# Retention gates and outputs with tokens on the partitions

## The chip, the cores and the metric

One core of one Trainium2 chip runs the whole program. The metric is device time in microseconds (us). Five engines work side by side, each in the order of its own instruction list: TensorE (PE in the profile, its weight loads PEld), VectorE (DVE), ScalarE (ACT), GpSimd (POOL) and SyncE (SP), which here only issues DMAs.

## The reference

Two layers over 256 tokens of 2048 features; layer 0 mixes tokens by retention, layer 1 by a short convolution, and each is followed by a SwiGLU. Everything is float32. What the change touches is the retention mixer:

```python
def retention_mixer(h, cos, sin, w_in, w_out):
    q, k, v, g = jnp.split(h @ w_in, [qk_w, 2 * qk_w, 2 * qk_w + v_w], axis=-1)
    q = rope(split_heads(q, RET_HEADS), cos, sin)
    k = rope(split_heads(k, RET_HEADS), cos, sin) * (RET_DK ** -0.5)
    v = split_heads(v, RET_HEADS)
    ...
    o = rms_norm(chunked_gated_linear_attention(q, k, v, log_a))
    o = merge_heads(o).astype(h.dtype)
    return ((jax.nn.silu(g) * o) @ w_out).astype(h.dtype)
```

There are 8 heads, with 256 features for q and k and 512 for v and g. The norm runs over the 512 outputs of one head and one token.

## The kernel before

**Layout.** Activations lie with features on the partitions and tokens along the free dimension: a tile of 128 features by 256 tokens. Float32 products are made from two rounded parts, `hi` (the value rounded) and `lo` (the rest), so one product takes three terms: hi x hi, hi x lo, lo x hi. `h[k]` holds both parts of feature block k.

**Weights.** All matrices lie in one array in the order of their use. `fetch` loads 1 MB pieces over SP's queue; `prepare` turns half a piece (1024 columns) into `hi` on ACT (L310) and `lo` on DVE (L313); `take` hands out the next 128 columns (512 for v). Up to two halves are prepared ahead, in four buffers each for `hi` and `lo`. TensorE streams through these pieces for nearly the whole span.

**Products.** A unit is one block of 128 weight columns for one k. `product` uses two matmuls per unit (L355 with 512 columns, L358 with 256). `packed` puts two column blocks in the two halves of one PSUM bank and uses three matmuls of 256 columns (L378 to L380); the weights stand still in the array and the tokens stream. `values` makes v the other way: the tokens stand still (two halves of 128) and 512 weight columns stream (L806 to L808), so that v comes out with tokens on the partitions. There are eight banks, each of 128 partitions by 512 values, and every call of `bank()` takes one.

**Retention.** While the modulation of layer 0 is still being computed, four spans (`SPANS`) already add up some k of q, k and g for heads 0 to 4 (19 to 191 us); `held` copies those sums to `ahead`. Then `projections` runs for the heads in the order 4, 0, 2, 1, 5, 3, 6, 7: q, k, v, `scores`, and the gates g in two groups of two column blocks, with SiLU on ACT (`gate`). After four heads, and after eight, `ret_out` multiplies by the output matrix.

**Asides.** The rest of a head, `mixed`, is cut into four steps that are put into TensorE's list between the units of the next head (or of `ret_out`): after 8, 8, 24 and 12 units (`STEPS`). `outputs(0)` and `outputs(1)` make two blocks each of 128 output features: four matmuls a block (L852, L855), `summed` (ACT copies one half of the bank, DVE adds the other: L387, L389), squares (ACT, L404, and DVE, L405), and a product with the gate (L860). `roots` sums the squares over the partitions on TensorE (L413), a small DVE operation takes the mean (L422), and POOL raises it to the power -1/2 (L424). `ends` spreads the factor over the partitions with TensorE (L431), multiplies (L869), and splits the result into `hi` and `lo` (L394 on ACT, L395 on DVE) as `mid`, the input of the output product.

**Order.** TensorE's list is in program order throughout. Outside of the start, the other engines' lists are ordered by the framework, which also puts in the waits. The rows of the modulation matrix are loaded and reduced on DVE (L244, 2.3 us each) at a pace that `paced` sets, with low priority.

Of the kernel before, what the change touches and what calls it, by code (L numbers as in the profile page):

```python
# [17 lines left out]
P = 128  # L18
# [27 lines left out]
MOD_LEAD = 64  # L46
MOST = 0.045
MOD_PRIO = -300
STEPS = (8, 8, 24, 12)
RAW_BUFS = 3  # L50
PART_BUFS = 4

# [4 lines left out]
class Group:  # L57


    def __init__(self, cols, width=P, ks=range(KT)):  # L60
        self.cols, self.width, self.ks = cols, width, list(ks)


def ret_in_groups():

    qkg, v = [], []
    for h in range(HEADS):  # L70
        q = [Q0 + h * DK + i * P for i in range(2)]
        k = [K0 + h * DK + i * P for i in range(2)]
        g = [G0 + h * DV + i * P for i in range(4)]
        qkg.append([q, k, g[:2], g[2:]])
        v.append(Group([V0 + h * DV], DV))
    done = [0] * HEADS
    spans = []
    for heads, (a, b) in SPANS:
        assert all(done[h] == a for h in heads)
        for h in heads:  # L80
            done[h] = b
        spans.append(Group([c for h in heads for pair in qkg[h] for c in pair], ks=range(a, b)))
# [73 lines left out]

def laid_out(arrays):

    total = sum(len(g.cols) * g.width * len(g.ks) for _, _, g in in_use_order())
    out = np.empty((total // CHUNK, P, CHUNK), np.float32)  # L160
    at = 0
    for key, i, g in in_use_order():
        for k in g.ks:
            for c in g.cols:
                o = at % CHUNK
                out[at // CHUNK, :, o : o + g.width] = arrays[key][i, k * P : (k + 1) * P, c : c + g.width]
                at += g.width
    assert at == total and total % CHUNK == 0
    return out

# [15 lines left out]
def trunk(ctx: ExitStack, tc: tile.TileContext, x_in, c_in, pos_in, w_mod, cols_in, tab_in, w_all, out):  # L186
# [75 lines left out]
    first = len(RET_SPANS[0].cols) * FIRST_KS  # L262
    early = sum(len(g.cols) * len(g.ks) for g in RET_SPANS)
    plan_mod = [(early, 0), (1024, 18), (1984, 49), (5184, 9 * KT), (5888, n_mod)]
    units, allowed = [0], [0.0]

# [14 lines left out]
            modulation(*todo.pop())  # L281


    order = [(g, k, c) for _, _, g in in_use_order() for k in g.ks for c in g.cols]
# [30 lines left out]

    prepared = [0]

    def take(group, k, col):

        assert order.pop() == (group, k, col)  # L320
# [9 lines left out]
        taken_cols[0] += group.width  # L330
        return [t[:, i : i + group.width] for t in ready[0]]

    def bank():
        return ps.tile([P, 2, S], F32, tag="bank", name=name("bank"))
# [10 lines left out]
    def product(g, act, base=0, before=None, banks=None, last=True):  # L345
# [16 lines left out]
        paced(len(g.cols) * len(g.ks))  # L362
        return banks

    def packed(g, act, base=0, before=None, between=None, banks=None):

        banks = banks or [bank() for _ in g.cols[::2]]
        for k in g.ks:
            if before:
                before(k)  # L370
            h = act[k - base]
            for i, c in enumerate(g.cols):
                if between and i == len(g.cols) // 2:
                    between(k)
                pt = banks[i // 2][:, i % 2, :]
                hi, lo = take(g, k, c)
                first, last = k == g.ks[0] and i % 2 == 0, k == g.ks[-1]
                nc.tensor.matmul(pt, hi, h[:, 0, :], start=first, stop=False, skip_group_check=True)  # L378
                nc.tensor.matmul(pt, hi, h[:, 1, :], start=False, stop=False, skip_group_check=True)  # L379
                nc.tensor.matmul(pt, lo, h[:, 0, :], start=False, stop=last, skip_group_check=True)  # L380
            ticked(len(g.cols))
        paced(len(g.cols) * len(g.ks))
        return banks

    def summed(pt, dst=None, at=slice(0, S)):
# [31 lines left out]
        return pt  # L417

    def norm_roots(pt, n):

        r = tmp("rs", (P, 2), bufs=4)
        nc.vector.tensor_scalar(r, pt[:, 0, 0:2], 1.0 / n, EPS, op0=ALU.mult, op1=ALU.add)  # L422
        r2 = tmp("rs", (P, 2), bufs=4)
        nc.gpsimd.tensor_tensor(r2, r, half, op=ALU.pow)  # L424
        return r2
# [117 lines left out]
    with ExitStack() as inner:  # L543
# [64 lines left out]
        with tc.tile_pool(name="start", bufs=1) as sp:  # L608
# [145 lines left out]
                step[0] += n / (2.0 * HEADS)  # L754

            def span(g):
                n = len(g.cols) // 2
# [34 lines left out]
            return dst  # L792

        def gate(s):
            g = rp.tile([P, S], F32, tag="sg", name=name("sg"), bufs=4)
            nc.scalar.activation(g, s, AF.Silu)
            return g

        def values(head, g):
            pts = [bank() for _ in range(2)]  # L800
            for k in range(KT):
                hi, lo = take(g, k, g.cols[0])
                for t, pt in enumerate(pts):
                    o = pt.rearrange("p a b -> p (a b)")
                    ht = h[k][:, :, t * P : (t + 1) * P]
                    nc.tensor.matmul(o, ht[:, 0, :], hi, start=k == 0, stop=False)  # L806
                    nc.tensor.matmul(o, ht[:, 0, :], lo, start=False, stop=False)  # L807
                    nc.tensor.matmul(o, ht[:, 1, :], hi, start=False, stop=k == KT - 1)  # L808
                ticked(4)
            paced(4 * KT)  # L810
# [30 lines left out]

        def mixed(head, both, v, sg):

            accs, os, pts = [None], [], []

            def outputs(half):
                for i in range(2 * half, 2 * half + 2):
                    pt = bank()
                    w = slice(i * P, (i + 1) * P)
                    for jt, sp in enumerate(both):  # L850
                        at = slice(jt * P, S)
                        nc.tensor.matmul(  # L852
                            pt[:, :, at], v[:, jt, 0, w], sp, start=jt == 0, stop=False, skip_group_check=True
                        )
                        nc.tensor.matmul(  # L855
                            pt[:, 1, at], v[:, jt, 1, w], sp[:, 0, :], start=False, stop=jt == 1, skip_group_check=True
                        )
                    o = summed(pt, rp.tile([P, S], F32, tag="o", name=name("o"), bufs=4))
                    accs[0] = squares(accs[0], o, "hacc")
                    nc.vector.tensor_tensor(o, o, sg[i], op=ALU.mult)  # L860
                    os.append(o)

            def roots():
                pts.append(norm_roots(norm_sums(accs), DV))

            def ends():
                rh = norm_spread(pts[0])
                for i, o in enumerate(os):
                    nc.vector.tensor_tensor(o, o, rh, op=ALU.mult)  # L869
                    n = 4 * head + i  # L870
                    mid[n] = rm_tile(("mid", n), F32R)
                    split(mid[n], o)

            return list(zip(STEPS, [lambda: outputs(0), lambda: outputs(1), roots, ends]))

        def pair(head, i):

            g = RET_HEADS[head][0][i]
            if not g.ks:
                return ahead[head, i]  # L880
            (pt,) = packed(g, h)
            if (head, i) in tag_of:
                free.append(tag_of.pop((head, i)))
            if (head, i) not in ahead:
                return pt
            s = tmp("qs", (P, 2, S), pool=rp, bufs=1)
            nc.vector.tensor_tensor(s, ahead[head, i], pt, op=ALU.add)
            return s

        def projections(head):  # L890
            q = rope(pair(head, 0), "q")
            k = rope(pair(head, 1), "k")
            v = values(head, RET_HEADS[head][1])
            sp = scores(head, q, k)
            s = pair(head, 2)
            sg = [gate(s[:, n, :]) for n in range(2)]
            s = pair(head, 3)
            sg += [gate(s[:, n, :]) for n in range(2)]
            asides.extend(mixed(head, sp, v, sg))
            since[0] = 0  # L900

# [127 lines left out]
```

## Time and profile before

| | us |
|---|---|
| three runs | 2656.36, 2658.65, 2659.3 |
| median | 2658.65 |
| the profiled execution | 2654.62 |
| its span, first to last instruction | 2652.8 |

The profile is that of the profiled execution. Its clock was 0.998 of full speed. Stages of the span, as far as they matter here: start until 19 us, spans of retention until 191, the heads until about 792 with the two output products at 345 to 439 and 704 to 792, then the first SwiGLU, the convolution and the second SwiGLU.

Instructions of the steps that the change touches, for all eight heads:

| line, engine | what | shape | times | mean ns |
|---|---|---|---|---|
| L378, L379, L380 PE | q, k and g, matmuls | 128x256 | 1024 each | 284, 283, 284 |
| L806, L807, L808 PE | v, matmuls | 128x512 | 256 each | 397, 394, 394 |
| L852 PE | outputs | 128x512 and 128x256 | 32 each | 425, 282 |
| L855 PE | outputs | 128x256 and 128x128 | 32 each | 280, 224 |
| L413 PE (hacc) | sums of squares | 128x1 | 32 | 229 |
| L431 PE | spread of factors, all norms | 128x128 | 52 | 300 |
| L389 DVE (o) | sum of the two halves | 128x256 | 32 | 418 (median) |
| L860, L869 DVE | products with gate and factor | 128x256 | 32 each | 421, 415 (median) |
| L394 ACT, L395 DVE (rm) | split of the result | 128x256 | 32 each | 402, 420 (median) |
| L424 POOL (heads) | power | 128x2 | 8 | 1712 (median), 689 to 4338 |

A row of the timeline gives the start in us, the duration in us, the engine and line, what is written from what, and in square brackets how long the engine was idle before it and what ended that. Matmuls overlap: one starts before the last has ended, so durations can't be added.

### The profile page before, as it was taken

How to read it: one execution, taken by the hardware profiler on the slowest of the kernel's cores; microseconds unless marked ns; L12 is line 12 of the kernel's file. 1: busy time of each engine (PE TensorE's matmuls, PEld its weight loads, DVE VectorE, ACT ScalarE, POOL GpSimd, SP SyncE). 2: the span in 40 equal slices, each digit the busy share in tenths (PEclk: the TensorE clock that was granted, in tenths of full speed). 3: DMA queues.
4: the chain of work that ended last, by engine and by line, in shares of the span. 5: the costliest groups of instructions: out<-in, count | busy, mean ns of one | idle time of the engine just before them, and what ended most of it. 6: DMA issues, size and time to landing. Idle time of an engine off the chain costs nothing.

```text
span 2652.8 us, 40070 instructions
## 1 busy us (share of the span) xinstructions
PE 2617.0 (99%) x16044; PEld 2335.4 (88%) x16044; DVE 2019.2 (76%) x2647; ACT 1259.6 (47%) x1818; POOL 152.9 (6%) x230
## 2 busy tenths in 40 slices
PE   7999999999999999999999999999999999999998
PEld 6998889999989888888888898888988888888887
DVE  7898888788698877777777889888887665555564
ACT  5545443444456444344444454444554443444443
POOL 0000101111000011101000001100000000000000
PEclk9999999999999999999999999999999999999999
DMA  9966668776676877777777758777776655544453
GB/s 397 392 275 248 229 237 312 264 263 263 250 272 251 325 280 263 293 276 280 280 279 267 284 216 324 288 268 271 265 262 265 255 222 191 190 185 185 188 189 127
DMA packets 96957, 687.69 MB, mean 259 GB/s; under 512 B 10753, under 2 KB 12545, under 8 KB 13825
## 3 DMA queue, kind: packets, MB, share of 16 engines
q1 hardware_dynamic: 96770, 685.13, 67.9%
q8 instruction: 125, 2.05, 0.3%
q14 instruction: 62, 0.51, 0.1%
HBM read 682.99 MB, written 2.10 MB: 258 GB/s over the span
## 4 chain that ended last, share of the span: by engine, by line
PE 76%; issue 19%; DVE 3%; DMA 1%; ACT 0%; POOL 0%; DVEq 0%; ACTq 0%; POOLq 0%
PE bank L355 34%; PE bank L358 18%; PE bank L380 4%; PE bank L378 4%; PE bank L379 4%; PE bank L806 2%; PE bank L808 2%; PE bank L807 2%; PE bank L494 1%; PE bank L493 1%; PE bank L495 1%; DMA raw<-w_mod 1%; DVE lo L313 1%; DVE raw L619 1%; PE bank L852 0%
## 5 line engine op out<-in xcount | busy, mean ns | idle before, releaser
L313 DVE TENSOR_TENSOR lo<-raw,hi 128x1024 fp32r<-128x1024 f32 x912 | 1113.2, 1224 | 537.9 <-ACT hi L310 532.0
L310 ACT CAST hi<-raw 128x1024 fp32r<-128x1024 f32 x912 | 953.2, 1050 | 1077.2 <-PE bank L355 658.4
L355 PE MATMUL bank<-h,hi 128*128 128x512 f32 x3296 | 1155.2, 395 | 0.0
L358 PE MATMUL bank<-h,lo 128*128 128x256 f32 x3296 | 926.2, 281 | 0.0
L355 PEld LDWEIGHTS bank<-h,hi 128*128 128x128 f32 x3296 | 623.0, 189 | 144.2
L358 PEld LDWEIGHTS bank<-h,lo 128*128 128x128 f32 x3296 | 623.3, 189 | 0.0
L355 PE MATMUL bank<-mid,hi 128*128 128x512 f32 x1604 | 556.3, 394 | 0.0
L358 PE MATMUL bank<-mid,lo 128*128 128x256 f32 x1604 | 445.4, 278 | 0.0
L244 DVE SCALAR_TENSOR_TENSOR raw<-raw,cb 128x2048 f32<-128x2048 f32 x160 | 365.7, 2285 | 11.9 <-DMA raw<-w_mod 11.9
L355 PEld LDWEIGHTS bank<-mid,hi 128*128 128x128 f32 x1604 | 301.1, 188 | 69.7
L358 PEld LDWEIGHTS bank<-mid,lo 128*128 128x128 f32 x1604 | 301.3, 188 | 0.0
L380 PE MATMUL bank<-h,lo 128*128 128x256 f32 x1024 | 290.8, 284 | 8.5 <-DVE lo L313 8.4
L378 PE MATMUL bank<-h,hi 128*128 128x256 f32 x1024 | 290.5, 284 | 2.5 <-ACT h L647 2.5
L379 PE MATMUL bank<-h,hi 128*128 128x256 f32 x1024 | 289.5, 283 | 0.5 <-DVE h L648 0.5
L380 PEld LDWEIGHTS bank<-h,lo 128*128 128x128 f32 x1024 | 193.9, 189 | 9.8 <-DVE lo L313 9.8
L378 PEld LDWEIGHTS bank<-h,hi 128*128 128x128 f32 x1024 | 195.8, 191 | 2.8 <-ACT h L647 2.8
L379 PEld LDWEIGHTS bank<-h,hi 128*128 128x128 f32 x1024 | 194.2, 190 | 0.8 <-DVE h L648 0.8
L355 PE MATMUL bank<-rm,hi 128*128 128x512 f32 x496 | 176.1, 400 | 0.2
L358 PE MATMUL bank<-rm,lo 128*128 128x256 f32 x496 | 139.5, 281 | 0.0
L355 PEld LDWEIGHTS bank<-rm,hi 128*128 128x128 f32 x496 | 93.3, 188 | 23.0 <-DVE rm L395 0.8
L806 PE MATMUL bank<-hi,h 128*128 128x512 f32 x256 | 101.7, 397 | 0.0
L807 PE MATMUL bank<-lo,h 128*128 128x512 f32 x256 | 101.0, 394 | 0.0
(156 smaller groups left out, 2188.2 us busy)
## 6 DMA issues: line engine op xcount, KB each, us to landing
raw<-w_all SPq DMA_DIRECT2D x456, 1024.0 KB, 4.9
raw<-w_mod SPq DMA_DIRECT2D x192, 1024.0 KB, 5.0
x<-x_in SPq DMA_DIRECT2D x4, 512.0 KB, 5.6
out<-out SPq DMA_DIRECT2D x5, 256.0 KB, 3.3
decay<-tab_in SPq DMA_DIRECT2D x8, 128.0 KB, 2.6
out<-out SPq DMA_DIRECT2D x3, 128.0 KB, 2.5
out<-out SPq DMA_DIRECT2D x1, 384.0 KB, 2.7
cols<-cols_in SPq DMA_DIRECT2D x1, 160.0 KB, 8.7
```

The source lines that it names most:

```text
L244: nc.vector.scalar_tensor_tensor(raw, raw, 1.0, cb, op0=ALU.mult, op1=ALU.mult, accum_out=total)
L310: nc.scalar.copy(hi, raw)
L313: nc.vector.tensor_tensor(lo, raw, hi.bitcast(F32), op=ALU.subtract)
L355: nc.tensor.matmul(pt, hi, h, start=fresh and k == g.ks[0], stop=False, skip_group_check=True)
L358: nc.tensor.matmul(pt[:, 1, :], lo, h[:, 0, :], start=False, stop=last and k == g.ks[-1], skip_group_check=True)
L378: nc.tensor.matmul(pt, hi, h[:, 0, :], start=first, stop=False, skip_group_check=True)
L379: nc.tensor.matmul(pt, hi, h[:, 1, :], start=False, stop=False, skip_group_check=True)
L380: nc.tensor.matmul(pt, lo, h[:, 0, :], start=False, stop=last, skip_group_check=True)
L493: nc.tensor.matmul(pt, hi, rows[0], start=k == 0, stop=False)
L806: nc.tensor.matmul(o, ht[:, 0, :], hi, start=k == 0, stop=False)
L807: nc.tensor.matmul(o, ht[:, 0, :], lo, start=False, stop=False)
L808: nc.tensor.matmul(o, ht[:, 1, :], hi, start=False, stop=k == KT - 1)
```

## The change

The gates and the outputs of a head are made with tokens on the partitions, as v already was.

- The four gate blocks of a head become one group of 512 columns (`items` in `Group` are pairs of column and width). `packed` meets such an item with `by_token`: per k, and for each half of the tokens, three matmuls of 512 columns into a bank of its own. `values` uses the same path.
- `gate` applies SiLU to a whole bank, twice a head.
- `outputs(t)` makes all 512 outputs of 128 tokens in one bank: three matmuls of 512 columns for t = 0 and six for t = 1. ACT squares the bank and sums along the free dimension into `total`, one column for each t.
- `normed_outputs` takes the factor from `total` as a value per partition, and one DVE instruction per t multiplies the bank by factor and gate. The sums over partitions (L413), the spread (L431) and the additions of squares are gone from this step.
- `ends` transposes the result on TensorE: for each of four blocks of 128 features two transposes of 128x128, one for each half of the tokens. Blocks 0 and 1 share one bank, blocks 2 and 3 another. The split reads the bank.
- `STEPS` becomes 8, 8, 20: the factor's chain follows `outputs(1)` at once, and `ends` comes 20 units later.

The core of the diff:

```diff
-STEPS = (8, 8, 24, 12)
+STEPS = (8, 8, 20)
...
-        g = [G0 + h * DV + i * P for i in range(4)]
-        qkg.append([q, k, g[:2], g[2:]])
+        qkg.append([q, k, [(G0 + h * DV, DV)]])
...
+    def by_token(banks, hi, lo, h, first, last):
+
+        for t, pt in enumerate(banks):
+            o = pt.rearrange("p a b -> p (a b)")
+            ht = h[:, :, t * P : (t + 1) * P]
+            nc.tensor.matmul(o, ht[:, 0, :], hi, start=first, stop=False)
+            nc.tensor.matmul(o, ht[:, 0, :], lo, start=False, stop=False)
+            nc.tensor.matmul(o, ht[:, 1, :], hi, start=False, stop=last)
...
+                if width == DV:
+                    by_token(banks[at // 2 : at // 2 + 2], hi, lo, h, k == g.ks[0], k == g.ks[-1])
+                    at += 4
+                    continue
...
         def gate(s):
-            g = rp.tile([P, S], F32, tag="sg", name=name("sg"), bufs=4)
+
+            g = rp.tile([P, 2, S], F32, tag="sg", name=name("sg"), bufs=2)
             nc.scalar.activation(g, s, AF.Silu)
-            return g
+            return g.rearrange("p a b -> p (a b)")
...
+            def outputs(t):
+
+                pt = bank().rearrange("p a b -> p (a b)")
+                pts.append(pt)
+                n = 0
+                for jt in range(t + 1):
+                    sp = both[jt][:, :, (t - jt) * P : (t - jt + 1) * P]
+                    for i, j in ((0, 0), (0, 1), (1, 0)):
+                        nc.tensor.matmul(pt, sp[:, i, :], v[:, jt, j, :], start=n == 0, stop=n == 3 * t + 2)
+                        n += 1
+                sq = rp.tile([P, DV], F32, tag="o", name=name("sq"), bufs=2)
+                nc.scalar.activation(sq, pt, AF.Square, accum_out=total[:, t : t + 1])
+
+            def normed_outputs():
+                r = roots_of(total, DV)
+                for t, pt in enumerate(pts):
+                    o = rp.tile([P, DV], F32, tag="o", name=name("o"), bufs=2)
+                    nc.vector.scalar_tensor_tensor(o, pt, r[:, t : t + 1], sg[t], op0=ALU.mult, op1=ALU.mult)
+                    os.append(o)
+
+            def last_outputs():
+                outputs(1)
+                normed_outputs()
+
+            def ends():
+                for i in range(4):
+                    if i % 2 == 0:
+                        pt = bank()
+                    for t, o in enumerate(os):
+                        nc.tensor.transpose(
+                            pt[:, i % 2, t * P : (t + 1) * P], o[:, i * P : (i + 1) * P], ident
                         )
...
                     n = 4 * head + i
                     mid[n] = rm_tile(("mid", n), F32R)
-                    split(mid[n], o)
-
-            return list(zip(STEPS, [lambda: outputs(0), lambda: outputs(1), roots, ends]))
+                    split(mid[n], pt[:, i % 2, :])
+
+            return list(zip(STEPS, [lambda: outputs(0), last_outputs, ends]))
```

More of the change, by code (lines that the diff above doesn't have):

```diff
@@ L60, in __init__ @@
     def __init__(self, cols, width=P, ks=range(KT)):
-        self.cols, self.width, self.ks = cols, width, list(ks)
+        self.items = [c if isinstance(c, tuple) else (c, width) for c in cols]
+        self.cols, self.ks = [c for c, _ in self.items], list(ks)
+        self.n = sum(w for _, w in self.items) // P
 def ret_in_groups():
@@ L81, in ret_in_groups @@
             done[h] = b
-        spans.append(Group([c for h in heads for pair in qkg[h] for c in pair], ks=range(a, b)))
+        spans.append(Group([c for h in heads for part in qkg[h] for c in part], ks=range(a, b)))
     rest = [[Group(c, ks=range(done[h], KT)) for c in qkg[h]] for h in range(HEADS)]
@@ L157, in laid_out @@
 def laid_out(arrays):
-    total = sum(len(g.cols) * g.width * len(g.ks) for _, _, g in in_use_order())
+    total = sum(g.n * P * len(g.ks) for _, _, g in in_use_order())
     out = np.empty((total // CHUNK, P, CHUNK), np.float32)
@@ L163, in laid_out @@
         for k in g.ks:
-            for c in g.cols:
+            for c, w in g.items:
                 o = at % CHUNK
-                out[at // CHUNK, :, o : o + g.width] = arrays[key][i, k * P : (k + 1) * P, c : c + g.width]
-                at += g.width
+                out[at // CHUNK, :, o : o + w] = arrays[key][i, k * P : (k + 1) * P, c : c + w]
+                at += w
     assert at == total and total % CHUNK == 0
@@ L261, in trunk @@
     todo.reverse()
-    first = len(RET_SPANS[0].cols) * FIRST_KS
-    early = sum(len(g.cols) * len(g.ks) for g in RET_SPANS)
+    first = RET_SPANS[0].n * FIRST_KS
+    early = sum(g.n * len(g.ks) for g in RET_SPANS)
     plan_mod = [(early, 0), (1024, 18), (1984, 49), (5184, 9 * KT), (5888, n_mod)]
@@ L281, in needed @@
             modulation(*todo.pop())
-    order = [(g, k, c) for _, _, g in in_use_order() for k in g.ks for c in g.cols]
+    order = [(g, k, c, w) for _, _, g in in_use_order() for k in g.ks for c, w in g.items]
     order.reverse()
@@ L316, in trunk, with take @@
     prepared = [0]
-    def take(group, k, col):
-        assert order.pop() == (group, k, col)
+    def take(group, k, col, width=P):
+        assert order.pop() == (group, k, col, width)
         i = taken_cols[0] % HALF
@@ L329, in take @@
                     break
-        taken_cols[0] += group.width
-        return [t[:, i : i + group.width] for t in ready[0]]
+        taken_cols[0] += width
+        return [t[:, i : i + width] for t in ready[0]]
     def bank():
@@ L363, in product @@
         return banks
+    def by_token(banks, hi, lo, h, first, last):
[5 more added lines that the diff above has]
+            nc.tensor.matmul(o, ht[:, 1, :], hi, start=False, stop=last)
     def packed(g, act, base=0, before=None, between=None, banks=None):
-        banks = banks or [bank() for _ in g.cols[::2]]
+        banks = banks or [bank() for _ in range((g.n + 1) // 2)]
         for k in g.ks:
@@ L371, in packed @@
             h = act[k - base]
-            for i, c in enumerate(g.cols):
-                if between and i == len(g.cols) // 2:
+            at = 0
+            for i, (c, width) in enumerate(g.items):
+                if between and i == len(g.items) // 2:
                     between(k)
-                pt = banks[i // 2][:, i % 2, :]
-                hi, lo = take(g, k, c)
-                first, last = k == g.ks[0] and i % 2 == 0, k == g.ks[-1]
+                hi, lo = take(g, k, c, width)
+                if width == DV:
+                    by_token(banks[at // 2 : at // 2 + 2], hi, lo, h, k == g.ks[0], k == g.ks[-1])
+                    at += 4
+                    continue
+                pt = banks[at // 2][:, at % 2, :]
+                first, last = k == g.ks[0] and at % 2 == 0, k == g.ks[-1]
                 nc.tensor.matmul(pt, hi, h[:, 0, :], start=first, stop=False, skip_group_check=True)
@@ L380, in packed @@
                 nc.tensor.matmul(pt, lo, h[:, 0, :], start=False, stop=last, skip_group_check=True)
-            ticked(len(g.cols))
-        paced(len(g.cols) * len(g.ks))
+                at += 1
+            ticked(g.n)
+        paced(g.n * len(g.ks))
         return banks
@@ L419, in norm_roots, with roots_of @@
     def norm_roots(pt, n):
+        return roots_of(pt[:, 0, 0:2], n)
+    def roots_of(total, n):
         r = tmp("rs", (P, 2), bufs=4)
-        nc.vector.tensor_scalar(r, pt[:, 0, 0:2], 1.0 / n, EPS, op0=ALU.mult, op1=ALU.add)
+        nc.vector.tensor_scalar(r, total, 1.0 / n, EPS, op0=ALU.mult, op1=ALU.add)
         r2 = tmp("rs", (P, 2), bufs=4)
@@ L794, in gate @@
         def gate(s):
-            g = rp.tile([P, S], F32, tag="sg", name=name("sg"), bufs=4)
+            g = rp.tile([P, 2, S], F32, tag="sg", name=name("sg"), bufs=2)
             nc.scalar.activation(g, s, AF.Silu)
-            return g
+            return g.rearrange("p a b -> p (a b)")
         def values(head, g):
[L800 to L810, printed above, removed]
+            pts = packed(g, h)
             v = rp.tile([P, 2, 2, DV], F32R, tag="v", name=name("v"))
@@ L842, in mixed @@
         def mixed(head, both, v, sg):
[L844 to L853, printed above, removed]
-                        )
[L855 to L869, printed above, removed]
+            total = tmp("osum", (P, 2), bufs=2)
+            pts, os = [], []
+            def outputs(t):
[9 more added lines that the diff above has]
+                nc.scalar.activation(sq, pt, AF.Square, accum_out=total[:, t : t + 1])
@@ L879, in pair @@
             if not g.ks:
[L880 to L888, printed above, removed]
+                return [ahead[head, n] for n in ((i,) if i < 2 else (2, 3))]
+            sums = packed(g, h)
+            for j, pt in enumerate(sums):
+                key = (head, i + j)
+                if key in tag_of:
+                    free.append(tag_of.pop(key))
+                if key in ahead:
+                    s = tmp("qs", (P, 2, S), pool=rp, bufs=1)
+                    nc.vector.tensor_tensor(s, ahead[key], pt, op=ALU.add)
+                    sums[j] = s
+            return sums
         def projections(head):
-            q = rope(pair(head, 0), "q")
-            k = rope(pair(head, 1), "k")
+            q = rope(*pair(head, 0), "q")
+            k = rope(*pair(head, 1), "k")
             v = values(head, RET_HEADS[head][1])
             sp = scores(head, q, k)
[L895 to L898, printed above, removed]
+            sg = [gate(s) for s in pair(head, 2)]
             asides.extend(mixed(head, sp, v, sg))
```

2 lines of the change are left out of this document (1 added, 1 removed).

## The prediction

> **What bounds the kernel now.** I read the engine totals first, then the chain of waits, then TensorE's instructions in order of time, since everything below is counted at their pace.
>
> ```profile
> PE 2617.0 (99%) x16044; PEld 2335.4 (88%) x16044; DVE 2019.2 (76%) x2647; ACT 1259.6 (47%) x1818; POOL 152.9 (6%) x230
> ```
>
> ```profile
> PE 76%; issue 19%; DVE 3%; DMA 1%; ACT 0%; POOL 0%; DVEq 0%; ACTq 0%; POOLq 0%
> ```
>
> TensorE has work 99% of the span, and 95% of the chain is PE or its issue. DVE (76%) and ACT (47%) have room, so what the change takes from them pays only where TensorE waits for them. TensorE runs in the order in which the program lists it: a wait in that list, or an instruction more, is lost time whole. The table of stretches gives the retention stage, 191 to 792 us:
>
> ```profile
> 191.00:792.00 601.00, 596.00 (x3751) 535.52 (x3750) 500.68 (x718) 282.52 (x418) 52.43 (x72) 1.00 0.69 259
> ```
>
> In that row the columns are PE, PEld, DVE, ACT and POOL busy, clock, DMA share, GB/s: PE 596 of 601 us, DVE 501, DMA 0.69. TensorE sets the end there, DMA does not.
>
> A matmul's duration includes its latency, so its price is the distance between starts. From TensorE's timeline:
>
> ```profile
> 185.00 0.28 PE L378 MATMUL bank<-h,hi 128*128 128x256 f32 x1
> ...
> 191.80 0.39 PE L806 MATMUL bank<-hi,h 128*128 128x512 f32 x1
> ...
> 199.92 0.40 PE L808 MATMUL bank<-hi,h 128*128 128x512 f32 x1
> ```
>
> 57 matmuls of 256 columns in 6.80 us: 0.119 each. 35 of 512 columns in 8.12 us: 0.232 each, less than twice 0.119. Now the work of one head around its outputs (head 0, in the values of head 2):
>
> ```profile
> 271.61 0.50 PE L413 MATMUL bank<-ones,hacc 128*128 128x1 f32 x4
> 271.97 0.48 PE L806 MATMUL bank<-hi,h 128*128 128x512 f32 x1
> ...
> 275.99 0.40 PE L808 MATMUL bank<-hi,h 128*128 128x512 f32 x1
> 278.47 0.71 PE L431 MATMUL bank<-tab,rs 128*128 128x128 f32 x4 [2.08 <-POOL rs L424]
> 278.93 0.48 PE L806 MATMUL bank<-hi,h 128*128 128x512 f32 x1
> ```
>
> The two sums over partitions take 0.36 us of TensorE (271.61 to 271.97), the two spreading products about as much, and here TensorE stood still for the power on POOL.
>
> **The change, part by part.** All sums are in TensorE time.
>
> Gates: per k and head 12 matmuls of 256 columns become 6 of 512: 12 x 0.119 - 6 x 0.232 = 0.04 us less. There are 128 such steps. The 40 at 19 to 150 us in the spans of heads 0 to 3 I count as nothing, because DMA is at 0.93 to 1.01 there and sets the pace; if that cover is gone they give 1.6 us more. 88 x 0.04 = **-3.5** (bounds -2.9, if head 4's span gains nothing either, and -5.1). No instruction is added and the weights come in the same chunks, so SP's queue is as before. Four SiLUs of 128x256 become two of 128x512: ACT, not on the path.
>
> Outputs: 16 matmuls, which take 2 x 1.12 us a head (708.52 to 709.65 for one half), become 9 of 512 columns, 9 x 0.232 = 2.09. 8 x 0.15 = **-1.2**.
>
> Norm: the sums and the spread go, 16 x 0.36 = **-5.8**. Copy, add, squares, two multiplications leave DVE and ACT (15 DVE instructions of 0.42 a head for two of about 0.8): hidden under TensorE, zero by itself.
>
> Transposes: eight a head, none in this trace. From below, an output 128 columns wide (L831) is followed by the next start after 0.06 us; from above, a spreading product is two instructions and takes 0.36 / 2 = 0.18. 64 x 0.06 = 3.8 to 64 x 0.18 = 11.6; I take 0.09, what one of the four instructions of the spread takes, since it has the same shape: **+5.8**. [...]
>
> The chain to the factor. Before, TensorE waited for POOL's power in three heads (at 272 to 278 us 2.3, at 525 to 531 us 1.6, at 324 us 0.3): 4.2 that go. Now the first transpose waits for: squares on ACT (about 1.1 after the last matmul: 0.5 until ACT is free, 0.59 as for the copy of 128x512 on L814), the small DVE operation and the power, two products of 128x512 on DVE (0.6 until DVE is free; 2 x 0.75, a little over the 0.69 of L783), 0.1 to start. From the sums' end to the power's end the eight heads of this trace took 2.6, 6.3, 4.3, 1.0, 5.6, 2.5, 2.5 and 1.0 us; with 3.3 added that is 4.3 to 9.6. 20 units of work cover 6.9 us (8.2 in the output product). Late are heads 0, 2 and 5 by 2.7, 0.7 and 2.0: 5.4. Net **+1.2**. Behind the waiting transpose stands all of TensorE.
>
> The bank between two transposed halves. This is the term that decides. `ends` asks for one bank for two column blocks: both token halves of block 0 are transposed into its first half, ACT copies that (`mid` hi), DVE subtracts from it (`mid` lo), and then block 1 is transposed into the other half of the same bank. In the order of the list that is write, read, read, write on one buffer. In the trace a bank is always filled whole before anything reads it; no row shows a write beside a read. So the price lies between nothing, if the halves are followed apart, and a full round: matmul end, ACT copy, DVE operation, TensorE again. The nearest rows are those of the old outputs, the same round on ACT and DVE in the same place:
>
> ```profile
> 709.59 0.23 PE L855 MATMUL bank<-sp,v 128*128 128x128 f32 x1
> 709.85 0.37 ACT L387 COPY low<-bank 128x256 f32<-128x256 f32 x1 [0.22 <-PE bank L855]
> 710.25 0.42 DVE L389 TENSOR_TENSOR o<-bank,low 128x256 f32<-128x256 f32 x1 [0.17 <-ACT low L387]
> ```
>
> ```profile
> 314.33 0.22 PE L855 MATMUL bank<-sp,v 128*128 128x128 f32 x1
> ...
> 316.64 1.22 DVE L313 TENSOR_TENSOR lo<-raw,hi 128x1024 fp32r<-128x1024 f32 x1
> 316.69 0.64 ACT L387 COPY low<-bank 128x256 f32<-128x256 f32 x2
> ...
> 318.38 0.76 DVE L389 TENSOR_TENSOR o<-bank,low 128x256 f32<-128x256 f32 x2
> ```
>
> The first takes 0.87 us from the matmul's end to DVE's end, the second 4.25, behind a `lo` of 1.22 and rope work; the 32 of the trace have a median of 1.9. With 0.2 for the transpose's own latency and 0.1 to start again that is 1.2 at best, 2.2 in the middle. I take 2.0, as DVE loses 15 x 0.42 - 1.6 = 4.7 us of work a head and TensorE's standstill lets it catch up. Two banks a head, eight heads: 16 x 2.0 = **+32** (19 to 48, that is 1.2 to 3.0 on average). Behind the waiting transpose stand the next weights' matmuls; ACT and DVE go on with `hi` and `lo` until the four buffers of each are full, and then SP's loads stop too, without harm at a DMA share of 0.69. I hold the wait for likely because the bank is one buffer, and the code does nothing to part its halves. [...]
>
> Sum: -3.5 - 1.2 - 5.8 + 5.8 + 1.2 + 32 = **+28.5**. The profiled execution took 2654.62 us (span 2652.8, 1.8 around it), 4.0 below the median 2658.65. From the one 2683.1, from the other 2687.2; I say **2686**.
>
> **The rivals.** (1) No wait at the bank: the second half is transposed while the first is read, 16 x 0. Then the sum is -3.5 and the time 2655, not slower; decided by whether the copy and the subtraction of block 0 end before or after block 1's transposes start. For it: the two halves share no data. Against it: one buffer. (2) The chain to the factor is late in every head, because POOL's power takes 0.69 to 4.34 us in this trace and DVE's two products stand behind a `lo` or a modulation reduction of 2.29. If every head is late as head 0 is, 8 x 2.7 = 21.6 in place of 5.4: +45, 2702. For it: three of eight are late by my own sum. Against it: DVE gets free time. (3) The clock. At the start, after waits of some us, 256-column matmuls start every 0.213 us until 24.3 us and then every 0.119, with the granted clock at 1.00 throughout: four us at that pace lose 1.8. If a chain wait and two bank waits in a row bring it back in each head, 8 x 1.8 = 14: 2700. Against it: after the wait of 2.08 at 278 us the pace is 0.232 at once. [...]
>
> **How the numbers follow.** A measurement of this kernel tells about 0.2%, 5.3 us, from no change. Chances: forecast 0.71, (1) 0.14, (2) 0.10, (3) 0.05. The forecast's own range is 2668 to 2706: waits of 1.2 to 3.0 give +15.7 to +44.5, the other bounds 3 to 6 more. To leave out no more than 2 in 10 the range has to hold (2) and (3) and need not hold (1): I widen it to 2660 to 2710. Faster by over 0.2% needs (1) and the cheap ends of gates and transposes: 0.07. Within 0.2%: the rest of (1), and waits near 0.5 us, 0.08. Slower: 0.85.
>
> **What would show it.** In the changed kernel: transposes whose idle time is ended by the DVE subtraction of the block before, about 2 us each, 16 times; TensorE idle in the retention stage some 35 us in place of 5; gate matmuls of 512 columns 0.232 apart; no L413 or L431 there; DVE busy some 38 us less over the stage. It is wrong if block 1's transposes follow block 0's without idle time, or if the copies start only after both blocks are transposed.

## The result, and the profile after

| | before | after |
|---|---|---|
| median of five runs, us | 2657.89 | 2682.92 |
| lowest to highest, us | 2656.36 to 2659.3 | 2679.15 to 2685.56 |
| the profiled execution, us | 2654.62 | 2684.12 |
| its span, us | 2652.8 | 2682.3 |
| TensorE instructions | 16044 | 15220 |

The ratio is 1.0093, with a 95% interval of 1.0079 to 1.0108: the change makes the kernel 25 us slower, although TensorE has 824 instructions less to do. The profiles are 29.5 us apart.

The engine totals of the changed kernel:

```profile
PE 2627.3 (98%) x15220; PEld 2303.8 (86%) x15220; DVE 1993.6 (74%) x2543; ACT 1248.4 (47%) x1770; POOL 145.8 (5%) x230
```

And its chain of waits:

```profile
PE 73%; issue 19%; DVE 4%; DMA 2%; ACT 1%; POOL 0%; DVEq 0%; ACTq 0%; POOLq 0%
```

TensorE still sets the end, but its share of the chain fell from 76 to 73% and DVE's rose by one. The row for the retention stage (PE, PEld, DVE, ACT, POOL busy, clock, DMA share, GB/s), now 191 to 820 us:

```profile
191.00:820.00 629.00, 602.74 (x3253) 517.41 (x3252) 473.97 (x611) 271.08 (x371) 42.35 (x72) 0.98 0.67 246
```

Two things are new in it: TensorE is idle for 26 us (629 - 603; 5 before), and the mean granted clock is 0.98 where it was 1.00. DVE is busy 27 us less. The waits of that stage, and the transposes (L890), show who is waited for:

```profile
PE bank L890 <- DVE rm L415: 26.3, 16, 2.5
```

The columns are us in total, times, and the longest: 16 waits, two for each head, each ended by the subtraction (L415) of the block before. There is no other wait of TensorE in the heads. The timeline of head 4's `ends`, with TensorE, ACT and DVE:

```profile
230.27 0.38 PE L890 MATMUL bank<-tab,o 128*128 128x128 f32 x2
230.28 1.22 DVE L315 TENSOR_TENSOR lo<-raw,hi 128x1024 fp32r<-128x1024 f32 x1
...
230.93 0.37 ACT L414 CAST rm<-bank 128x256 fp32r<-128x256 f32 x1
231.42 0.69 DVE L814 TENSOR_TENSOR k<-qa,k 128x512 fp32r<-128x512 f32 x1
232.02 0.42 DVE L415 TENSOR_TENSOR rm<-bank,rm 128x256 fp32r<-128x256 f32 x1
...
232.50 0.66 PE L890 MATMUL bank<-tab,o 128*128 128x128 f32 x4 [1.85 <-DVE rm L415]
...
234.30 0.69 PE L890 MATMUL bank<-tab,o 128*128 128x128 f32 x2 [1.14 <-DVE rm L415]
234.64 0.78 PE L372 MATMUL bank<-hi,h 128*128 128x512 f32 x1
...
235.64 0.63 PE L374 MATMUL bank<-hi,h 128*128 128x512 f32 x1
236.06 0.63 PE L372 MATMUL bank<-hi,h 128*128 128x512 f32 x1
```

Block 0 is transposed at 230.27, copied at 230.93, and its subtraction stands on DVE behind a `lo` and a step of the rope until 232.02; only then come block 1 and, in the next bank at once, block 2. Block 3 waits again. After that the weights' matmuls of 512 columns start 0.42 us apart instead of 0.23. The stretches of 3.4 us around it (columns as above) show why:

```profile
227.20:230.60 3.40, 3.40 (x16) 2.56 (x15) 3.40 (x8) 1.44 (x3) 0.00 (x0) 1.00 0.71 289
230.60:234.00 3.40, 0.71 (x5) 0.42 (x4) 3.40 (x6) 1.34 (x4) 0.00 (x0) 1.00 0.01 2
234.00:237.40 3.40, 3.10 (x9) 2.52 (x10) 0.67 (x2) 0.37 (x1) 0.00 (x0) 0.51 0.80 263
237.40:240.80 3.40, 3.40 (x16) 2.76 (x15) 2.09 (x2) 1.40 (x2) 0.00 (x0) 0.99 0.13 51
```

Here a stretch in which TensorE worked 0.71 of 3.4 us is followed by one at half the granted clock (0.51), with 9 matmuls in it instead of 16. In the clock record this happens once in or after the `ends` of each of the eight heads, for 3.41 us each. The record has two more such stretches, at 42.9 and 155.5 us, before the heads; the record of before, at a mean clock of 0.998, has none there.

### The profile page after: what moved, and what is told of

The parts are those of the page before. It is cut to its first block, busy times and chain, and to the rows that moved or that the text cites. A ratio compares the mean times of both kernels' runs of the same rounds, so it can differ in the third digit from the quotient of the medians.

```text
span 2682.3 us, 38239 instructions
## 1 busy us (share of the span) xinstructions
PE 2627.3 (98%) x15220; PEld 2303.8 (86%) x15220; DVE 1993.6 (74%) x2543; ACT 1248.4 (47%) x1770; POOL 145.8 (5%) x230
## 3 DMA queue, kind: packets, MB, share of 16 engines
q8 instruction: 119, 1.95, 0.3%
## 4 chain that ended last, share of the span: by engine, by line
PE 73%; issue 19%; DVE 4%; DMA 2%; ACT 1%; POOL 0%; DVEq 0%; ACTq 0%; POOLq 0%
PE bank L357 34%; PE bank L360 17%; PE bank L372 4%; PE bank L373 4%; PE bank L374 4%; PE bank L399 2%; PE bank L397 2%; PE bank L398 2%; PE bank L517 1%; PE bank L516 1%; PE bank L518 1%; DVE lo L315 1%; DMA raw<-w_all 1%; DVE raw L642 1%; DMA raw<-w_mod 1%
## 5 line engine op out<-in xcount | busy, mean ns | idle before, releaser
L360 PE MATMUL bank<-h,lo 128*128 128x256 f32 x3296 | 924.4, 280 | 0.0
L357 PEld LDWEIGHTS bank<-h,hi 128*128 128x128 f32 x3296 | 622.5, 189 | 145.3
L360 PEld LDWEIGHTS bank<-h,lo 128*128 128x128 f32 x3296 | 622.0, 189 | 0.0
L372 PE MATMUL bank<-hi,h 128*128 128x512 f32 x512 | 206.1, 403 | 0.0
L373 PE MATMUL bank<-lo,h 128*128 128x512 f32 x512 | 205.3, 401 | 0.0
L374 PE MATMUL bank<-hi,h 128*128 128x512 f32 x512 | 205.0, 400 | 0.0
L399 PE MATMUL bank<-h,lo 128*128 128x256 f32 x512 | 147.1, 287 | 6.8 <-DVE lo L315 6.8
L397 PE MATMUL bank<-h,hi 128*128 128x256 f32 x512 | 146.9, 287 | 2.5 <-ACT h L670 2.5
L398 PE MATMUL bank<-h,hi 128*128 128x256 f32 x512 | 146.5, 286 | 0.5 <-DVE h L671 0.5
L374 PEld LDWEIGHTS bank<-hi,h 128*128 128x128 f32 x512 | 98.4, 192 | 23.4
L372 PEld LDWEIGHTS bank<-hi,h 128*128 128x128 f32 x512 | 98.7, 193 | 20.2
L373 PEld LDWEIGHTS bank<-lo,h 128*128 128x128 f32 x512 | 98.3, 192 | 20.1
```

The lines of the kernel that those rows point to most:

```text
L357: nc.tensor.matmul(pt, hi, h, start=fresh and k == g.ks[0], stop=False, skip_group_check=True)
L360: nc.tensor.matmul(pt[:, 1, :], lo, h[:, 0, :], start=False, stop=last and k == g.ks[-1], skip_group_check=True)
L372: nc.tensor.matmul(o, ht[:, 0, :], hi, start=first, stop=False)
L374: nc.tensor.matmul(o, ht[:, 1, :], hi, start=False, stop=last)
```

## The experiments

**The transposes first.** Is the order at the bank the loss?

```diff
             def ends():
+                banks = [bank() for _ in range(2)]
                 for i in range(4):
-                    if i % 2 == 0:
-                        pt = bank()
                     for t, o in enumerate(os):
                         nc.tensor.transpose(
-                            pt[:, i % 2, t * P : (t + 1) * P], o[:, i * P : (i + 1) * P], ident
+                            banks[i // 2][:, i % 2, t * P : (t + 1) * P], o[:, i * P : (i + 1) * P], ident
                         )
+                for i in range(4):
                     n = 4 * head + i
                     mid[n] = rm_tile(("mid", n), F32R)
-                    split(mid[n], pt[:, i % 2, :])
+                    split(mid[n], banks[i // 2][:, i % 2, :])
```

> All eight transposes of a head come first, then the four splits, so no bank is written again after it was read; nothing else differs. Theory (the rounds at the bank, 26.3 us in the profile, and the half clock that follows them, about 8 x 1.5 us, are the whole loss): no wait on DVE rm before a transpose, granted clock 1.00 after the ends of every head, and the time falls below the kernel before: gates -3.5, outputs -2.8 with the wait at head 4, norm -6.1, POOL waits -4.2, transposes +5 to +10, spans -1, so 2646 to 2652. Rival A (the transposes do not count as work for the clock and bring the half clock by themselves): the waits go but the clock still falls in each head, 2658 to 2664. Rival B (the wait is for the products on DVE, not for the bank): 2680 or more, as in the changed kernel.

Measured: 2643.4 us median, before 2655.59 beside it, ratio 0.9956 (0.9944 to 0.9969). The row of its retention stage (columns as above):

```profile
191.00:790.00 599.00, 599.00 (x3343) 519.10 (x3342) 480.44 (x626) 274.52 (x377) 50.48 (x74) 1.00 0.73 265
```

TensorE waits for nothing between 191 and 790 us, and the clock is 1.00. In the timeline the eight transposes of head 4 are one row without idle time, and the next matmul starts 0.79 us later:

```profile
232.07 1.03 PE L889 MATMUL bank<-tab,o 128*128 128x128 f32 x8
232.86 0.48 PE L372 MATMUL bank<-hi,h 128*128 128x512 f32 x1
```

The whole loss hung on the order of transposes and splits: by the medians the same instructions in another order are 39.5 us faster than the changed kernel (1.4% by the ratios), and faster than the kernel before. Rivals A and B are out.

**Blocks 1 and 3 later.** Is it the second write to the bank that costs, or the round not being covered?

```diff
-STEPS = (8, 8, 20)
+STEPS = (8, 8, 20, 12)
...
             def ends():
...
+                pair_of.extend(bank() for _ in range(2))
+                block(0)
+                block(2)
+
+            def rest():
+                block(1)
+                block(3)
+
+            return list(zip(STEPS, [lambda: outputs(0), last_outputs, ends, rest]))
```

Here `block(i)` is the body of the old loop.

> The bank is still written, read and written again, but blocks 1 and 3 are transposed 12 units of work after blocks 0 and 2. Theory: the round at the bank (1 to 2.5 us) lies under 4.3 us of matmuls, so hardly a wait is left, the clock stays at 1.00, and the time is that of the kernel with the transposes first, 2646 to 2653. Rival (what costs is a second write to a bank, not the time of the round): 2675 to 2685.

Measured: 2642.32, ratio 0.9953 (0.9937 to 0.9968), and one wait of 0.2 us is left at the transposes. The bank is still written, read and written again, but the round lies under 12 units of matmuls: what costs is a round that nothing covers. This one and the former can't be told apart in time.

**The gates alone.** Outputs, norm and ends as before the change; the gate then meets outputs of the other layout, so that product is not the reference's.

```diff
-STEPS = (8, 8, 20)
+STEPS = (8, 8, 24, 12)
...
-                        nc.tensor.matmul(pt, sp[:, i, :], v[:, jt, j, :], start=n == 0, stop=n == 3 * t + 2)
...
+                        nc.tensor.matmul(
+                            pt[:, :, at], v[:, jt, 0, w], sp, start=jt == 0, stop=False, skip_group_check=True
+                        )
...
+                    nc.vector.tensor_tensor(o, o, sg[i // 2][:, (i % 2) * S : (i % 2 + 1) * S], op=ALU.mult)
```

> Only the gates come with tokens on the partitions; outputs, norm and ends are those of the kernel before (the gate then meets outputs in the other layout, so the values are not the reference's). Theory: 88 steps of 0.04 us in the heads are saved, and up to 40 more in the spans: 2653 to 2655, the clock at 1.00 in the heads, POOL waits as before. Rival (the gates bring something of the loss, by two banks at once or by the spans, where the clock fell twice in the changed kernel): 2658 or more.

Measured: 2653.9, ratio 0.9996 (0.9987 to 1.0005): no change that can be told. The time lies in the range expected, but the kernel before was 2.3 us lower beside it than in the table above, so the gain is 1.1 us by the ratio where 88 x 0.04 = 3.5 was expected. The profile shows where part of it went: the wait at the first outputs of head 4 is 1.7 (1.4 before), and a wait of 2.28 us for POOL in the values of head 3 is followed by a stretch at half clock. Two more stretches at half clock, at 42.4 and 155.0 us, lie in the spans. The profile of every run here with the new gates has one or two such stretches between 42 and 161 us; those of the kernel before and of the outputs alone, with the old gates, both at a mean clock of 0.998, have none. That the new gates bring them is not shown: the mean clock of this profile was 0.996, and other executions of the kernel before were at 0.996 and 0.997 too. The first scores of head 4 start 0.8 us later than before (214.9 and 214.1). By pace the saving is there: 12 x 0.1193 - 6 x 0.2328 = 0.035 us a step.

**Three rounds a bank.** Each transpose is split at once, for 128 tokens.

```diff
-                    for t, o in enumerate(os):
-                        nc.tensor.transpose(
-                            pt[:, i % 2, t * P : (t + 1) * P], o[:, i * P : (i + 1) * P], ident
-                        )
                     n = 4 * head + i
                     mid[n] = rm_tile(("mid", n), F32R)
-                    split(mid[n], pt[:, i % 2, :])
+                    for t, o in enumerate(os):
+                        at = slice(t * P, (t + 1) * P)
+                        nc.tensor.transpose(pt[:, i % 2, at], o[:, i * P : (i + 1) * P], ident)
+                        nc.scalar.copy(mid[n][:, 0, at], pt[:, i % 2, at])
...
```

> The split follows each transpose at once, for 128 tokens, so each bank is written after a read three times and not once: 48 rounds instead of 16. Theory: 48 x 1.2 to 1.6 = 58 to 77 us of waits instead of 26, and the clock at half speed for two windows a head instead of one (+1.5 x 8): 2725 to 2755. Rival (the wait is for the products on DVE): 2680 to 2690.

Measured: 2726.95 in one run. The waits of TensorE at the transposes (total us, times, longest):

```profile
PE bank L893 <- DVE rm L895: 51.9, 48, 4.0
```

48 waits for 48 rounds, so there is one for every write after a read. Each is 1.1 on average: a bare round on 128 columns leaves 0.68 idle (31 of the 48), the rest, behind other work on ACT or DVE, 0.8 to 4.0. The time lies at the lower end of what was expected, because the bare rounds are shorter than I had put them. The clock was expected at half speed for two stretches a head; it was there for three in a row, 10.24 us in each of the eight heads (mean clock 0.983).

**Ten times the transposes.** Does the half clock come from transposes or from standing still? The diff is against the kernel with the transposes first.

```diff
-                for i in range(4):
+                for i in list(range(4)) * 10:
```

> As the kernel with the transposes first, but each transpose is done ten times: 80 back to back in each head instead of 8, without idle time. It asks whether the half clock of the changed kernel came from standing still or from transposes. Theory (standing still): the granted clock stays at 1.00 after the 80 transposes, and the time grows by 72 x 8 x 0.06 to 0.10 = 35 to 58 us, to 2678 to 2701. Rival (transposes do not count as work for the clock): 80 x 0.06 to 0.10 is 4.8 to 8 us, longer than a window of 3.4 us, so the clock falls in all eight heads, transposes included, and the time is at least 8 x 1.4 us more.

Measured: 2703.67 in one run. Rows of the stretches around the `ends` of two heads, 80 transposes from 228.9 to 237.6 and from 274.7 to 283.3:

```profile
231.00:235.00 4.00, 4.00 (x39) 4.00 (x38) 0.67 (x1) 0.00 (x0) 0.00 (x0) 1.00 0.55 172
235.00:239.00 4.00, 4.00 (x32) 3.77 (x31) 2.38 (x3) 0.74 (x2) 0.00 (x0) 1.00 0.22 92
239.00:243.00 4.00, 4.00 (x18) 3.22 (x18) 2.58 (x5) 2.52 (x4) 0.19 (x1) 1.00 0.77 252
277.00:281.00 4.00, 4.00 (x39) 4.00 (x38) 2.14 (x6) 0.62 (x1) 0.00 (x0) 1.00 0.75 262
```

The clock is 1.00 during and after 8.66 us of nothing but transposes, in all eight heads (mean clock 0.998). A transpose takes 0.108 us of the stream, more than the 0.06 to 0.10 expected, and so the time lies 2.7 us above the range of the theory. The rival is out: 80 float32 transposes in a row kept the clock at 1.00. Whether they also bring the clock back from half speed, no run here shows.

**Early ends.** And does standing still in one piece bring the half clock without a round at a bank? Again against the kernel with the transposes first.

```diff
-STEPS = (8, 8, 20)
+STEPS = (8, 8, 4)
```

> As the kernel with the transposes first, but they come 4 units after the second outputs instead of 20, so TensorE waits in one piece for the factor and the products on DVE. In the trace of the former kernel 5.0 us pass from the last output matmul to the end of the second product (head 4); 4 units cover 1.4. Theory (standing still brings the half clock): one wait of 3 to 4.5 us a head for DVE o, the clock falls in at least four of the eight heads though only eight transposes of 0.8 us follow, and the time is 2643 + 8 x 3.5 + 1.4 x 4 to 8 = 2677 to 2683 (2668 to 2692 with the spread of the waits). Rival (idle time broken up by transposes is needed): the clock stays at 1.00, 2671.

Measured: 2671.87 in one run. TensorE waits 16.4 us in total for the products on DVE, 0.8 to 3.1 a head, less than expected. So the time is near the rival's 2671, but the clock (mean 0.994) decides against the rival: it falls in four of the eight heads, after single waits of 1.8 to 2.9 us. One wait of 1.9 us, in another head, left it at 1.00. The transposes of head 4 in the timeline:

```profile
227.77 2.32 PE L889 MATMUL bank<-tab,o 128*128 128x128 f32 x8 [2.79 <-DVE o L878]
```

And the stretches around them:

```profile
223.70:227.10 3.40, 1.28 (x6) 0.71 (x4) 2.81 (x6) 1.13 (x3) 2.20 (x1) 1.00 0.28 84
227.10:230.50 3.40, 2.61 (x10) 2.25 (x11) 3.40 (x8) 0.75 (x3) 0.00 (x0) 0.50 0.73 299
```

A stretch with 1.28 us of work is followed by half clock. So idle time in one piece, without a round at a bank, brought it here, with 2.12 of the 3.40 us idle. In this head the half clock lasts for two stretches, to 233.9 us, though TensorE was busy for 2.61 us of the first, mostly with transposes. The run also sizes the chain to the factor: from the end of the last output matmul to the end of the second product it takes 3.2 to 4.8 us in the eight heads, where 20 units cover 6.9.

**The outputs alone.** Gates projected as before, the rest as with the transposes first; the gate meets outputs of the other layout here too.

```diff
-        qkg.append([q, k, [(G0 + h * DV, DV)]])
+        g = [G0 + h * DV + i * P for i in range(4)]
+        qkg.append([q, k, g[:2], g[2:]])
...
-            sg = [gate(s) for s in pair(head, 2)]
+            sg = [gate(s) for i in (2, 3) for s in pair(head, i)]
```

> The gates are projected as in the kernel before (four blocks of 128 features), outputs, norm and transposes as in the kernel with the transposes first (the gate then meets outputs in the other layout, so the values are not the reference's). Theory: the gain is that of the outputs, the norm and the waits that go: outputs -1.4, norm -6.1, POOL waits -4.2, wait at head 4 -1.4, transposes +6.3, fewer breaks in the output product -2.2: -9, 2645 to 2649, and 3.5 more than with the gates changed too. Rival (the gain needs the gates): 2652 or more.

Measured: 2647.34, ratio 0.9971 (0.996 to 0.9983), 7.8 us by the medians: most of the gain is that of the outputs. With the gates too it is 0.9956, some 4 us more, but the two intervals overlap, and the gates alone showed 1.1.

**Two pieces.** The changed order, with its 16 rounds, but blocks 2 and 3 come 12 units after 0 and 1.

```diff
-STEPS = (8, 8, 20)
+STEPS = (8, 8, 20, 12)
...
-            return list(zip(STEPS, [lambda: outputs(0), last_outputs, ends]))
+            return list(zip(STEPS, [lambda: outputs(0), last_outputs, lambda: ends(0), lambda: ends(2)]))
```

> The order of transposes and splits is the changed kernel's, with its 16 rounds at the banks, but blocks 2 and 3 come 12 units after blocks 0 and 1, so no window of 3.4 us is mostly idle. Theory (two causes: the rounds, 16 x 1.9 = 30, and the half clock, 8 x 1.4 = 11): the rounds stay, 26 us of idle time on TensorE, the clock stays at 1.00, and the time is 2643 + 30 = 2669 to 2677. Rival (each round lowers the clock, or the clock costs nothing): 2680 to 2686, as the changed kernel.

Measured: 2690.6, ratio 1.0137 (1.0121 to 1.0152): slower than the changed kernel, and outside both ranges expected. The rounds stayed, but each became longer, 33.0 us of idle time instead of 26.3, and the clock still fell, in five places, in one of them for two stretches. One of them:

```profile
235.66 1.04 ACT L312 CAST hi<-raw 128x1024 fp32r<-128x1024 f32 x1 [1.77 <-PE bank L374]
236.61 0.36 ACT L414 CAST rm<-bank 128x256 fp32r<-128x256 f32 x1
236.73 1.23 DVE L315 TENSOR_TENSOR lo<-raw,hi 128x1024 fp32r<-128x1024 f32 x1 [1.59 <-ACT hi L312]
237.88 0.42 DVE L415 TENSOR_TENSOR rm<-bank,rm 128x256 fp32r<-128x256 f32 x1
...
238.35 0.56 PE L890 MATMUL bank<-tab,o 128*128 128x128 f32 x2 [2.57 <-DVE rm L415]
```

The copy stands behind a `hi` of 1.04 and the subtraction behind a `lo` of 1.23: the copy starts at 236.61 as the `hi` ends, the subtraction at 237.88 as the `lo` ends, and TensorE stands still for 2.57. In the changed kernel the second round of a head often found ACT and DVE empty, since TensorE had just stood still; apart, the second wait of a head is longer in six of the eight (1.9 to 2.6 us). Of the nine waits of 2.4 to 4.2 us, five were followed by the half clock. The run therefore doesn't part the two causes in time; their sizes rest on the starts of TensorE's instructions, below.

## Why the prediction came out

The table gives TensorE's time from the first scores of head 4 to the first matmul of the SwiGLU, by the distance from each start to the next, summed over the instructions of each step.

| | before | after | transposes first |
|---|---|---|---|
| q, k, v, gates | 369.29 | 368.27 | 360.11 |
| scores | 8.99 | 8.98 | 8.99 |
| outputs | 17.91 | 16.55 | 16.55 |
| sums and spread of the norm | 6.11 | | |
| `ends` | | 36.61 | 6.34 |
| output products | 181.79 | 182.71 | 179.61 |
| sum | 584.10 | 613.12 | 571.59 |

The differences of the sums are 29.0 for the changed kernel and -12.5 for the one with the transposes first; the change in the spans ahead is smaller than 2.5 us in all kernels here. Step by step:

| step | forecast | measured |
|---|---|---|
| gates | -3.5 | -2.5 by the pace: 72 of the 88 steps lie in this stage, of 0.035 each |
| outputs | -1.2 | -1.4 |
| norm | -5.8 | -6.1 |
| transposes | +5.8 | +6.3: 64 x 0.099 |
| chain to the factor | +1.2 | -3.9: the waits for POOL go (2.2, 1.5 and 0.2 by the starts, 4.2 in the prediction), none comes |
| rounds at the banks | +32 | +30.3: 36.61 - 6.34, 1.9 each |
| half clock | 0 (rival, 14) | +11.3: the rows of after without `ends`, less those of transposes first |
| not in the sum | 0 | -1.4, the wait of head 4's outputs for its scores; about -3.5 left over |

Of what is left over, 2.2 us lie in the output products: with the transposes first their matmuls of 512 columns start 0.234 us apart on average, before the change 0.237. Why is not shown.

**What was right.** The mechanism that decides, its place and its size: a wait for DVE's subtraction before every second block, 16 times, 1.9 us each with TensorE's own latency (2.0 forecast). The prices of gates, outputs, norm and transposes were right within 1 us each, all from distances between starts in the trace of before. The first rival, no wait, fell with the first line of the waits, and with the 48 waits for 48 rounds. In the changed kernel's trace no transpose started before the readers of the other half were done, 16 waits of 0.9 to 2.5 us. The framework put in these waits, so the runs show what its order costs, and not what the chip would do without it.

**What was mis-sized.** Two terms, of opposite sign. The first is the chain to the factor: I had taken the old power times and added 3.3, and found three heads late. From the end of the last output matmul to the end of the second product the changed kernel took 3.2 to 5.0 us, where the forecast had 4.3 to 9.6. The power's median on POOL fell from 1712 to 712 ns, and the transposes came 1.8 to 5.2 us after the products were ready; the second rival falls with it.

The second is the clock: it was a rival of its own with a chance of 0.05, ruled out by one row of before (a wait of 2.08 us, pace unchanged at once). That row showed one wait; two waits of 0.9 to 2.5 close together left 0.66 to 1.60 us of work in the stretch of 3.41 us before the fall, and the clock fell in eight heads of eight. In before, the stretches counted back in steps of 3.413 us from the one fall of its record (2642.35 us, in the last work of the span) cut the wait of 2.08 in two, and the one with less work (276.9 to 280.3) kept some 1.85 us. The clock's loss came on top of the rounds, not in place of them, and its price, 1.4 a head, is near the 1.8 that I had worked out from the start of the trace.

The total of 28.5 thus came near the 29.0 of this stage by luck: the clock loss, left out, made up for gains that were not counted, 5.1 at the chain, 1.4 at head 4 and about 3.5 left over. Two of the signs came smaller than forecast. TensorE was idle for 26 us and not 35: the chain brought none of its 5.4, and of the 1.9 a round some 0.25 is no idle time (30.3 / 16 less 26.3 / 16); I put it down to TensorE's own latency. DVE was relieved of 27 us and not 38: its instructions overlap too, two of 0.42 take 0.76 in a row, so 15 of them are some 5.1 us in a row and not 6.3.

**What the rest shows.** The layout does not lose by itself: with the transposes first it is 0.44% faster than before (0.9956, 0.9944 to 0.9969).

## What to carry to other kernels

A bank that is filled in two goes should be filled whole before anything reads it, or the second go should come some units of work later: here one order of the same instructions is 39.5 us from the other. The round trip to two busy engines cost what stood in their queues here, not the two instructions alone: TensorE stood still for 0.68 us when the round was bare (three rounds a bank), and for up to 4.2 (two pieces). Where the engine that sets the end stands still, count the half clock beside the wait: in the changed kernel 0.66 to 1.60 us of work in a stretch of 3.41 was followed by it in eight heads of eight, at 1.4 us a head.

## What the runs showed of the hardware that was not expected

- The granted clock fell to one half for 3.41 us, or two or three times that, after stretches of 3.4 us with 0.71 (changed kernel, 230.6 to 234.0), 0.83 (two pieces, 235.1 to 238.5), 1.28 (early ends, 223.7 to 227.1) and 1.39 us of work (gates alone, 527.1 to 530.5). In the changed kernel the falls lie whole multiples of 3.413 us apart (234.04 and 278.41 us: 13). Counted in stretches of that length from the falls, the most work that was followed by a fall there was 1.60 us in the heads (377.4 to 380.8) and 1.95 in the last work of the span (2667.7 to 2671.2), while 1.80 (271.6 to 275.0) and 1.81 (374.0 to 377.4) kept the clock. No one amount of work that parts the two is shown.
- From half clock, a stretch with 2.61 us of work (early ends, 227.1 to 230.5) was followed by another at half, and one with 2.98 (changed kernel, 541.2 to 544.7) by full clock.
- Float32 transposes of 128x128 followed each other every 0.099 us (transposes first) to 0.108 us (ten times), and in both runs the clock stayed at 1.00 through them. Each is one instruction in the trace (L890, 64 for 64 transposes) where a float32 product of that shape shows two (L431 before, 4 for the two of a spread).
- The power on POOL, two columns in all, took 0.69 to 4.34 us before and 0.69 to 2.20 after; why was not tried.
